# A four-layer hybrid trunk on one core: start order, first weight unit, unit loop, logits order, memory norm and recurrence order changed

## The chip, the cores and the metric

The kernel runs on one core of one Trainium2 chip. The metric is the device time of one execution in microseconds. Inputs and outputs are float32: 256 tokens of width 1024, 256 memory tokens, four layers.

## The reference

Four residual layers; each has a mixer (differential attention, HGRN2 recurrence, chunked SGU, differential attention), a cross-attention into the normed memory and a SwiGLU feed-forward. What the change touches, cut from the reference:

```python
mem_n = rmsnorm(mem, norm_mem)
...
for i in range(DEPTH):
    hn = rmsnorm(x, norm_mix[i])
    mix = (diff_attention, hgrn2, chunked_sgu)[i % 3](hn, ...)
    x = x + mix
    x = x + mem_cross_attention(rmsnorm(x, norm_cross[i]), mem_n, ...)
    x = x + swiglu(rmsnorm(x, norm_ffn[i]), ...)
# diff_attention: 8 heads, two 64-wide q and k per head
lam = exp(sum(lq1 * lk1)) - exp(sum(lq2 * lk2)) + lam_init
p = softmax(logits)                      # logits per head and feature half c
attn = p[:, :, 0] - lam * p[:, :, 1]
# hgrn2: A[t, s] = sum_k q[t] * k[s] * prod of the gates between s and t
```

## The kernel before, in words

**Weights.** All projections stream their weights in units of 1 MB. `load_to` (DMA issue at L116, on the SP queue, which starts transfers in program order) fills a ring of three raw buffers; `split_to` turns a unit into a rounded half `whi` (ScalarE cast, L132) and a remainder `wlo` (VectorE subtract, L133), each in two pieces of 128x1024. One float32 product is three matmuls: high by high, high by low, low by high.

**Two kinds of blocks.** `columns_steps` (L221, L226) takes 256 weight columns per unit and makes transposed results, `join` (L240, L241) copies them out of PSUM. `rows_steps` (L172) takes 256 weight rows per unit and accumulates into four PSUM banks, one for each token tile `t` and column half `n`; in a unit its loops run over `kk`, then `t`, then `n`. Both are generators that yield after each matmul.

**Hand order.** In differential attention and in the recurrence TensorE's order is written by hand: `advance(filler, n)` issues the next n steps of the projections, and between them stand the small pieces, `weigh` (logits at L562, bias and scale L567, softmax L571 to L587), `turn` (transposes of the attention), `near` and `level` of the recurrence. The other engines are ordered by a scheduler, except where `keep_in_program_order` pins an instruction.

**Start.** `run` transposes x in two halves (`norm_half`: sums of squares on ScalarE, L290, and transposes L267 with copies L256, L257) and splits the first unit. The four lambda vectors, each broadcast to 128 partitions, come over ScalarE's queue; two VectorE products use them (L397). `memory` norms mem (sums L290, L417, power on GpSimd L285, scaling L421), transposes it (16 matmuls, L267) and splits it; it is called in layer 0 before the q block.

**Logits.** The two feature halves c sit on partitions 0 to 63 and 64 to 127; for each token tile and head the two halves' matmuls follow each other, into banks `pl0` and `pl1`.

**Recurrence.** `level(lev, hq)` for eight levels and two head quarters (L777 products into `psa`, then L784, L785, L790 scalings and the masked copy L793); `near` prepares the next level's operand `hke` (L750, L752). Single calls of `level` alternate with 9 filler steps.

## Time and profile before

| | |
|---|---|
| median of 3 runs | 1633.71 us (1633.59 to 1634.44) |
| the profiled execution | 1635.31 us, span 1633.6 us |
| matmul records on TensorE | 8221 |
| mean granted TensorE clock | 0.994 |
| HBM traffic | 283 MB, 173 GB/s over the span |

The span is from the first to the last instruction. Slices of the profile's page show TensorE in nine tenths or more of every slice but the first and the last, with the clock at nine tenths or more in every slice but the first; times below are microseconds from the span's start. The clock of a window is in the windows' rows: 1.00 is 2.4 GHz, 0.50 is 1.2 GHz.

### The profile page before, as it was taken

Reading aid. Unit: us, or ns where it says so; the run is one execution under the profiler, and the core shown is the slowest. Engines: PE = TensorE matmul, PEld = TensorE weight load, DVE = VectorE, ACT = ScalarE, POOL = GpSimd, SP = SyncE. Lnnn points to the kernel's source line nnn. Section 1 sums busy time; section 2 is a strip of 40 time slices with the busy share of each in tenths; the row PEclk is TensorE's granted clock in tenths of the full one; section 3 lists DMA queues with packets and bytes.
Section 4 is the critical chain, followed back from the end, with each engine's and each line's share of the span. In section 5 each row is a group of like instructions: output and inputs, shape, how many; then the busy total and the mean of one; then the engine's idle time right before and its main releaser. Section 6 shows DMA issues by size and latency. Waiting matters only on the chain.

```text
span 1633.6 us, 21253 instructions
## 1 busy us (share of the span) xinstructions
PE 1607.5 (98%) x8221; PEld 1359.5 (83%) x8221; DVE 1022.7 (63%) x1482; ACT 880.7 (54%) x1467; POOL 43.5 (3%) x86
## 2 busy tenths in 40 slices
PE   6999999999999999999999999999999999999998
PEld 5788888888888888888888888888888788888886
DVE  5877765554687667555545866555547876665463
ACT  5676554453564656454436655544535765554452
POOL 2000000000000000000000000000000000000000
PEclk8999999999999999999999999999999999999999
DMA  8535445556543454564565554455656455455461
GB/s 290 183 125 192 163 154 181 185 179 203 181 155 104 140 172 154 162 199 155 206 206 170 192 181 155 155 184 165 218 182 205 129 172 186 141 183 183 134 236 68
DMA packets 151253, 282.87 MB, mean 173 GB/s; under 512 B 6390, under 2 KB 79840, under 8 KB 151024
## 3 DMA queue, kind: packets, MB, share of 16 engines
q1 hardware_dynamic: 146368, 275.34, 51.2%
q10 hardware_dynamic: 4320, 4.47, 0.9%
q0 software_dynamic: 464, 1.70, 0.3%
q8 instruction: 64, 1.05, 0.3%
q14 instruction: 37, 0.30, 0.1%
HBM read 280.43 MB, written 2.63 MB: 173 GB/s over the span
## 4 chain that ended last, share of the span: by engine, by line
PE 93%; DVE 1%; ACT 1%; issue 0%; POOL 0%; DVEq 0%; POOLq 0%; ACTq 0%
PE acc L172 67%; PE acc L221 11%; PE acc L226 6%; PE pst L267 3%; PE psa L777 1%; PE pso L980 1%; PE psl L941 1%; PE pl L562 0%; DVE wlo L133 0%; PE pse L964 0%; DVE de L567 0%; DVE dmx L571 0%; PE pso L626 0%; ACT de L577 0%; PE pso L627 0%
## 5 line engine op out<-in xcount | busy, mean ns | idle before, releaser
L133 DVE TENSOR_TENSOR wlo<-wraw,whi 128x1024 fp32r<-128x1024 f32 (+1 forms) x536 | 635.4, 1191 | 439.5 <-ACT whi L132 435.2
L132 ACT CAST whi<-wraw 128x1024 fp32r<-128x1024 f32 (+1 forms) x536 | 547.6, 1026 | 528.4 <-PE acc L172 467.3
L172 PE MATMUL acc<-whi,xs 128*128 128x512 f32 x1728 | 546.2, 393 | 2.2 <-DVE dq L241 2.1
L172 PEld LDWEIGHTS acc<-whi,xs 128*128 128x128 f32 x1728 | 324.4, 188 | 70.4 <-DVE dq L241 3.5
L172 PE MATMUL acc<-wlo,xs 128*128 128x512 f32 x864 | 338.4, 392 | 0.0
L221 PE MATMUL acc<-xs,whi 128*128 128x512 f32 x704 | 251.4, 401 | 7.9 <-ACT whi L132 6.9
L226 PE MATMUL acc<-xs,wlo 128*128 128x256 f32 x704 | 197.7, 284 | 0.0
L172 PEld LDWEIGHTS acc<-wlo,xs 128*128 128x128 f32 x864 | 162.7, 188 | 32.3
L221 PEld LDWEIGHTS acc<-xs,whi 128*128 128x128 f32 x704 | 133.6, 191 | 38.3 <-ACT whi L132 7.1
L172 PE MATMUL acc<-wlo,hh 128*128 128x512 f32 x352 | 137.5, 391 | 0.0
L172 PE MATMUL acc<-whi,hh 128*128 128x512 f32 x352 | 137.4, 392 | 0.0
L226 PEld LDWEIGHTS acc<-xs,wlo 128*128 128x128 f32 x704 | 134.8, 192 | 1.7 <-DVE wlo L133 0.8
L172 PE MATMUL acc<-whi,hl 128*128 128x512 f32 x352 | 112.0, 390 | 0.0
L172 PE MATMUL acc<-wlo,oh 128*128 128x512 f32 x256 | 100.6, 393 | 0.0
L172 PE MATMUL acc<-whi,oh 128*128 128x512 f32 x256 | 100.3, 392 | 0.0
L221 PE MATMUL acc<-m,whi 128*128 128x512 f32 x256 | 89.8, 394 | 0.0
L172 PE MATMUL acc<-whi,ol 128*128 128x512 f32 x256 | 84.8, 392 | 0.0
L172 PE MATMUL acc<-whi,m 128*128 128x512 f32 x256 | 80.7, 392 | 0.0
L172 PEld LDWEIGHTS acc<-whi,hh 128*128 128x128 f32 x352 | 66.1, 188 | 14.4 <-DVE ftmp L1007 1.1
L172 PEld LDWEIGHTS acc<-whi,hl 128*128 128x128 f32 x352 | 66.1, 188 | 13.6
L172 PEld LDWEIGHTS acc<-wlo,hh 128*128 128x128 f32 x352 | 66.1, 188 | 13.4
L226 PE MATMUL acc<-m,wlo 128*128 128x256 f32 x256 | 71.8, 280 | 0.0
(235 smaller groups left out, 1712.7 us busy)
## 6 DMA issues: line engine op xcount, KB each, us to landing
wraw<-in_ffn_w_gu_dram SPq DMA_DIRECT2D x160, 512.0 KB, 4.4
wraw<-in_ffn_w_down_dram SPq DMA_DIRECT2D x44, 1024.0 KB, 4.9
wraw<-in_ca_w_kv_dram SPq DMA_DIRECT2D x32, 1024.0 KB, 5.2
wraw<-in_da_w_in_dram SPq DMA_DIRECT2D x24, 1024.0 KB, 5.2
wraw<-in_ca_w_q_dram SPq DMA_DIRECT2D x16, 1024.0 KB, 5.2
wraw<-in_ca_w_o_dram SPq DMA_DIRECT2D x16, 1024.0 KB, 4.9
wraw<-in_hg_w_in_dram SPq DMA_DIRECT2D x16, 1024.0 KB, 5.5
wraw<-in_da_w_out_dram SPq DMA_DIRECT2D x8, 1024.0 KB, 4.9
```

What stands on the lines that cost most here:

```text
L132: nc.scalar.copy(h, rq)
L133: nc.vector.tensor_tensor(l, rq, h.bitcast(F32), op=ALU.subtract)
L172: nc.tensor.matmul(acc[key], lhsT=x_(k)[:, t * P : (t + 1) * P], rhs=w_[kk][:, 0, c], start=first and j == 0, stop=last and j == 2,)
L221: nc.tensor.matmul(acc[j].rearrange("p (s t) -> p s t", s=2), lhsT=wh[k // 4][:, k % 4, c], rhs=x[:, :, k, :], start=k == 0, stop=False, s ...
L226: nc.tensor.matmul(acc[j][:, 0:256], lhsT=wl[k // 4][:, k % 4, c], rhs=x[:, 0, k, :], start=False, stop=k == 7, skip_group_check=True,)
L267: nc.tensor.transpose(ps[:, i * 256 + t * P : i * 256 + (t + 1) * P], src[:, t, cs * P : (cs + 1) * P], self.ident)
L777: nc.tensor.matmul(ps[:, o : o + 64].rearrange("p (b e) -> p b e", e=half), lhsT=kes[lev % 2][:, h, t * P : (t + 1) * P], rhs=right, start ...
L941: nc.tensor.matmul(ps[:, t * 256 : (t + 1) * 256], lhsT=q_[:, 2 * h + d, t * P : (t + 1) * P], rhs=k_[:, 2 * h + d, :], start=n == 0, stop ...
L980: nc.tensor.matmul(pso[:, d * 256 : (d + 1) * 256], lhsT=v_[:, m, c], rhs=e_[:, h, m, :], start=n == 0, stop=n == 5)
```

## The change

Seven edits. (1) The four lambda transfers go from ScalarE's queue to SP's, behind mem, and the two products are pinned in program order. (2) The first weight unit is loaded by two transfers of 512 KB; the loop's variable `n` is also `load_to`'s argument, so a call stops earlier than asked. (3) `run` transposes both halves of x before any sum of squares. (4) In a unit of `rows_steps` the token tile is the outer loop. (5) The logits' matmuls run by feature half, then token tile. (6) `memory` is called inside the q block of layer 0, after 32 of its steps, with its sums pinned. (7) In the recurrence both head quarters of a level follow each other, then 24 filler steps. What is cut from the diff only moves sums of squares into functions of their own.

```diff
--- before.py
+++ after.py
@@ -113,7 +113,10 @@
             r = self.pw.tile([P, nk, width], F32, tag="raw", bufs=N_RAW, name="wraw")
             o = 0
             for src, cw in parts:
-                nc.sync.dma_start(out=r[:, :, o : o + cw], in_=src.rearrange("(k p) n -> p k n", p=P))
+                n = 2 if self.n_load == 0 else 1
+                for q in range(n):
+                    ks = slice(q * nk // n, (q + 1) * nk // n)
+                    nc.sync.dma_start(out=r[:, ks, o : o + cw], in_=src.rearrange("(k p) n -> p k n", p=P)[:, ks, :])
                 o += cw
             self.raw[self.n_load] = r
             self.n_load += 1
@@ -178,9 +181,9 @@
             if mid is not None and u == at:
                 mid()
             wh, wl = self.next_unit()
-            for kk in range(2):
-                k = 2 * u + kk
-                for t in range(2):
+            for t in range(2):
+                for kk in range(2):
+                    k = 2 * u + kk
                     for n in range(nn):
                         for j in range(2):
                             mm((t, n), k, kk, wh, wl, (j,))
@@ -316,17 +319,17 @@
         self.load_to(N_RAW)
         self.mem = self.slab(3, [P, 2, D], name="mem")
         nc.sync.dma_start(out=self.mem, in_=a["mem"][0].rearrange("(t p) d -> p t d", p=P))
-
         self.st = self.slab(8, [P, 1152], name="start")
+        lq = self.st[:, 0:512].rearrange("p (a l d) -> p a l d", a=4, l=2)
+        for i, n in enumerate(("da_lq1", "da_lk1", "da_lq2", "da_lk2")):
+            nc.sync.dma_start(out=lq[:, i], in_=a[n].partition_broadcast(P))
+
         rel = self.small([8, BUCKETS], "rel", bufs=1)
         nc.gpsimd.dma_start(out=rel, in_=a["rel_bias"])
         tb = self.st[:8, 768:1152]
         nc.gpsimd.memset(tb[:, 256:384], NEG)
         g1 = self.slab(10, [P, P], name="g1")
         nc.scalar.dma_start(out=g1[0:32, :], in_=a["norm_mix"].rearrange("l (c p) -> (l c) p", p=P))
-        lq = self.st[:, 0:512].rearrange("p (a l d) -> p a l d", a=4, l=2)
-        for i, n in enumerate(("da_lq1", "da_lk1", "da_lq2", "da_lk2")):
-            nc.scalar.dma_start(out=lq[:, i], in_=a[n].partition_broadcast(P))
         self.g1b = self.slab(13, [P, P], name="g1b")
         for i, g in enumerate((a["norm_cross"], a["norm_ffn"], a["hg_lower_bounds"])):
             nc.gpsimd.dma_start(out=self.g1b[i * 32 : (i + 1) * 32, :], in_=g.rearrange("l (c p) -> (l c) p", p=P))
@@ -394,7 +397,7 @@
         lq = st[:, 0:512].rearrange("p (a l d) -> p a l d", a=4, l=2)
         pr = st[:, 512:768].rearrange("p (a l d) -> p a l d", a=2, l=2)
         for i in range(2):
-            nc.vector.tensor_tensor(pr[:, i], lq[:, 2 * i], lq[:, 2 * i + 1], op=ALU.mult)
+            self.tc.keep_in_program_order(nc.vector.tensor_tensor(pr[:, i], lq[:, 2 * i], lq[:, 2 * i + 1], op=ALU.mult))
         ls = self.small([P, 4], "lqs", bufs=1)
         nc.vector.tensor_reduce(ls, pr.rearrange("p a l d -> p (a l) d"), axis=AX.X, op=ALU.add)
         nc.scalar.activation(ls, ls, AF.Exp)
@@ -412,7 +415,8 @@
         ss = self.small([P, 2, 2], "ss", bufs=2)
         for t in range(2):
             for n in range(2):
-                self.sumsq(ss[:, t, n : n + 1], self.mem[:, t, n * 512 : (n + 1) * 512])
+                ins = self.sumsq(ss[:, t, n : n + 1], self.mem[:, t, n * 512 : (n + 1) * 512])
+                self.tc.keep_in_program_order(ins)
         st = self.small([P, 2], "sst", bufs=2)
         nc.vector.tensor_reduce(st, ss, axis=AX.X, op=ALU.add)
         r = self.small([P, 2], "rstd", bufs=2)
@@ -531,7 +541,6 @@
         nc.vector.tensor_scalar_mul(sc, rstd, 0.125)
         if l == 0:
             self.more_consts()
-            self.memory()
         aT1 = self.slab(13, [P, 8, 256], name="daT1")
         aT0 = self.slab(14, [P, 8, P], name="daT0")
         s0 = self.small([P, 4, 2, 2], "ds0", bufs=1)
@@ -554,15 +563,16 @@
             mx = self.small([P, 2, 4], "dmx", bufs=3)
             sm = self.small([P, 2, 2, 2], "dsm", bufs=3)
             hs = slice(2 * hp, 2 * hp + 2)
-            for t, w in tiles:
-                lg = [self.ps("pl0"), self.ps("pl1")]
-                for i in range(2):
-                    for c in range(2):
-                        r = slice(c * 64, (c + 1) * 64)
+            lgs = [[self.ps("pl0"), self.ps("pl1")] for _ in tiles]
+            for c in range(2):
+                r = slice(c * 64, (c + 1) * 64)
+                for (t, w), lg in zip(tiles, lgs):
+                    for i in range(2):
                         nc.tensor.matmul(
                             lg[c][:, i * w : (i + 1) * w], lhsT=qt[r, 2 * hp + i, t * P : (t + 1) * P],
                             rhs=kt[r, 2 * hp + i, 0:w], start=True, stop=True,
                         )
+            for (t, w), lg in zip(tiles, lgs):
                 for c in range(2):
                     nc.vector.scalar_tensor_tensor(
                         e[t][:, c], lg[c][:, : 2 * w].rearrange("p (h m) -> p h m", h=2), sc[:, t : t + 1],
@@ -603,8 +613,11 @@
         es = {}
         advance(filler, 16)
         self.load_bias(bias)
+        advance(filler, 16)
+        if l == 0:
+            self.memory()
         for n, act, hp in (
-            (44, weigh, 0), (48, weigh, 1), (8, turn, 0), (32, weigh, 2),
+            (28, weigh, 0), (48, weigh, 1), (8, turn, 0), (32, weigh, 2),
             (8, turn, 1), (28, weigh, 3), (8, turn, 2), (26, turn, 3),
         ):
             advance(filler, n)
@@ -803,20 +816,14 @@
 
         filler = both()
         with self.in_order():
-            advance(filler, 96)
-            near(0, 0)
-            advance(filler, 16)
-            level(0, 0)
-            advance(filler, 24)
-            level(1, 0)
-            advance(filler, 16)
-            near(0, 1)
-            advance(filler, 12)
-            for i in range(14):
-                level(*((i // 2, 1) if i % 2 == 0 else (2 + i // 2, 0)) if i < 12 else (i - 6, 1))
-                if i == 1:
-                    corner()
-                advance(filler, 9 if i < 11 else 16)
+            advance(filler, 128)
+            for hq in range(2):
+                near(0, hq)
+            for lev in range(8):
+                advance(filler, 24 if lev else 18)
+                for hq in range(2):
+                    level(lev, hq)
+            corner()
             advance(filler, 320)
         o = self.slab(9, [P, 2, D], name="ho")
         psos, later = [], []
@@ -1061,9 +1068,13 @@
         self.make_plan()
         self.consts()
         self.begin_norm(5, self.g_mix(0))
-        self.norm_half(0)
-        self.split_to(1)
-        self.norm_half(1)
+        for n in range(2):
+            self.transpose_split(self.x, self.xh, self.xl, [(c, c) for c in range(4 * n, 4 * n + 4)], self.xgain)
+            if n == 0:
+                self.split_to(1)
+        for n in range(2):
+            self.norm_sums(n)
+            self.norm_power(n)
         for l in range(DEPTH):
             mixer = (self.diff_attention, self.hgrn2, self.sgu)[l % 3]
             mixer(l, lambda mid: self.mem_k(l, mid))
```

Line numbers in the pieces of order below are those of each kernel's own file: what is L116, L132, L133, L240, L241 before is L119, L135, L136, L243, L244 now, and L172, L221, L226 are L175, L224, L229.

**VectorE at the start**, before: `start` is the tile with the lambda vectors, `xs` the transposed x, `wraw`, `whi`, `wlo` the weight unit and its parts.

```order
L356 COPY G<-psg 128x32
L397 TENSOR_TENSOR start<-start 128x128 x2
L399 TENSOR_REDUCE lqs<-start 128x4
L257 SCALAR_TENSOR_TENSOR xs<-pst,G,xs 128x256 x3
L133 TENSOR_TENSOR wlo<-wraw,whi 128x1024
L257 SCALAR_TENSOR_TENSOR xs<-pst,G,xs 128x256
L133 TENSOR_TENSOR wlo<-wraw,whi 128x1024
```

The same place now:

```order
L359 COPY G<-psg 128x32
L260 SCALAR_TENSOR_TENSOR xs<-pst,G,xs 128x256
L136 TENSOR_TENSOR wlo<-wraw,whi 128x1024
L260 SCALAR_TENSOR_TENSOR xs<-pst,G,xs 128x256 x2
L136 TENSOR_TENSOR wlo<-wraw,whi 128x1024
L260 SCALAR_TENSOR_TENSOR xs<-pst,G,xs 128x256 x3
L136 TENSOR_TENSOR wlo<-wraw,whi 128x1024
L260 SCALAR_TENSOR_TENSOR xs<-pst,G,xs 128x256 x2
```

The lambda products and their sum stood second; they are gone from here to the end of the key block. **SP at the start**, before:

```order
L309 DMA ident<-in_c_ident_dram 128x128
L313 DMA x<-in_x_dram 128x512 x2
L116 DMA wraw<-in_da_w_in_dram 128x8x256 x3
L318 DMA mem<-in_mem_dram 128x2x1024
L116 DMA wraw<-in_da_w_in_dram 128x8x256 x5
L116 DMA wraw<-in_da_w_in_dram 128x2x1024 x4
```

and now:

```order
L312 DMA ident<-in_c_ident_dram 128x128
L316 DMA x<-in_x_dram 128x512 x2
L119 DMA wraw<-in_da_w_in_dram 128x4x256 x2
L119 DMA wraw<-in_da_w_in_dram 128x8x256
L321 DMA mem<-in_mem_dram 128x2x1024
L325 DMA start<-in_da_lq_dram 128x128
L325 DMA start<-in_da_lk_dram 128x128
L325 DMA start<-in_da_lq_dram 128x128
L325 DMA start<-in_da_lk_dram 128x128
L119 DMA wraw<-in_da_w_in_dram 128x8x256 x6
```

The first unit is two transfers, the third unit stands behind mem and the lambda vectors.

**TensorE and ScalarE in the q block of layer 0**, TensorE before (`g1b` and `g` are gains, `acc` the projections' banks):

```order
L221 MATMUL acc<-xs,whi 128x512
L226 MATMUL acc<-xs,wlo 128x256
L365 MATMUL psg<-ident,g1b 128x96
L369 MATMUL psg<-ident,g_104 128x19
L267 MATMUL pst<-ident,mem 128x128 x16
L221 MATMUL acc<-xs,whi 128x512
L226 MATMUL acc<-xs,wlo 128x256
```

TensorE now:

```order
L224 MATMUL acc<-xs,whi 128x512
L229 MATMUL acc<-xs,wlo 128x256
L224 MATMUL acc<-xs,whi 128x512
L229 MATMUL acc<-xs,wlo 128x256
L270 MATMUL pst<-ident,mem 128x128 x16
L224 MATMUL acc<-xs,whi 128x512
L229 MATMUL acc<-xs,wlo 128x256
```

ScalarE now, around the sums over mem (`dq` is the q block's result, `lbe` and `lqs` belong to bounds and lambda):

```order
L385 ACTIVATE lbe<-lbe 128x32
L135 CAST whi<-wraw 128x1024
L243 COPY dq<-acc 128x256 x2
L293 ACTIVATE junk,ss<-mem 128x512
L135 CAST whi<-wraw 128x1024
L403 ACTIVATE lqs<-lqs 128x4
L293 ACTIVATE junk,ss<-mem 128x512 x3
L259 ACTIVATE m<-pst,G_437 128x256 x8
```

The 16 transposes of mem move from the start of the q block to the end of its first unit; ScalarE's four sums over mem stand behind the copies of that same unit's result.

**VectorE before the first two levels of the recurrence**, before (`hks`, `hk`, `hq`, `hf` are shifted key, key, query, gate; `psa` a level's products):

```order
L724 TENSOR_TENSOR hks<-hk,hf 128x2x255
L241 TENSOR_TENSOR hf<-acc,hf 128x256
L767 TENSOR_TENSOR hb<-hf 128x4x127
L716 TENSOR_TENSOR hf<-hf,rb 128x512
L785 TENSOR_TENSOR hks<-hks,hf 128x4x127
L133 TENSOR_TENSOR wlo<-wraw,whi 128x1024
L719 TENSOR_SCALAR hf<-hf,lb 128x256 x2
L784 TENSOR_TENSOR hq<-hq,hf 128x512
L723 TENSOR_SCALAR hk<-hf 128x512
L793 COPY_PREDICATED hA<-masks,psa 128x256
L724 TENSOR_TENSOR hks<-hk,hf 128x2x255
```

and now:

```order
L737 TENSOR_TENSOR hks<-hk,hf 128x2x255
L729 TENSOR_TENSOR hf<-hf,rb 128x512
L136 TENSOR_TENSOR wlo<-wraw,whi 128x1024
L732 TENSOR_SCALAR hf<-hf,lb 128x256 x2
L798 TENSOR_TENSOR hks<-hks,hf 128x4x127
L736 TENSOR_SCALAR hk<-hf 128x512
L797 TENSOR_TENSOR hq<-hq,hf 128x512
L737 TENSOR_TENSOR hks<-hk,hf 128x2x255
L806 COPY_PREDICATED hA<-masks,psa 128x256 x2
L780 TENSOR_TENSOR hb<-hf 128x4x127
L798 TENSOR_TENSOR hks<-hks,hf 128x4x127
```

The scaling of the first quarter's query (now L797), which rewrites what the first level's matmuls read, stands ahead of the last quarter of shifted keys (now L737).

## Rows read from the trace of the kernel before

**Rows 1.** The page, busy time of TensorE: us (share of the span) x instructions.

```profile
PE 1607.5 (98%) x8221; PEld 1359.5 (83%) x8221; DVE 1022.7 (63%) x1482; ACT 880.7 (54%) x1467; POOL 43.5 (3%) x86
```

**Rows 2.** TensorE's waits, by line and releaser: us in total, times, longest us.

```profile
PE acc L221 <- ACT whi L132: 6.9, 1, 6.9
...
PE acc L172 <- DVE dq L241: 2.1, 2, 1.8
```

**Rows 3.** Timeline of VectorE at the start: start, us, instruction, [idle before <-releaser].

```profile
11.66 0.29 DVE L397 TENSOR_TENSOR start<-start 128x128 f32<-128x128 f32 x1 [4.90 <-DMA start<-in_da_lk_dram]
...
14.21 0.29 DVE L397 TENSOR_TENSOR start<-start 128x128 f32<-128x128 f32 x1 [2.26 <-DMA start<-in_da_lk_dram]
```

**Rows 4.** Timeline of TensorE at the start.

```profile
6.46 3.48 PE L267 MATMUL pst<-ident,x 128*128 128x128 f32 x16
...
16.84 1.22 PE L221 MATMUL acc<-xs,whi 128*128 128x512 f32 x2 [6.90 <-ACT whi L132]
```

**Rows 5.** Windows: busy (x) of PE PEld DVE ACT POOL, clock, DMA, GB/s.

```profile
16.84:23.20 6.36, 6.32 (x19) 4.93 (x20) 5.92 (x11) 6.36 (x13) 1.27 (x2) 0.50 1.08 408
...
23.20:44.00 20.80, 20.80 (x123) 18.11 (x123) 17.84 (x30) 14.03 (x26) 0.70 (x1) 1.00 0.92 296
...
77.90:81.30 3.40, 3.40 (x13) 2.37 (x13) 2.06 (x2) 0.81 (x1) 0.00 (x0) 0.50 0.35 86
...
470.40:473.80 3.40, 3.40 (x12) 2.93 (x12) 3.17 (x7) 0.45 (x1) 0.00 (x0) 0.50 0.07 28
...
1269.00:1271.00 2.00, 1.22 (x7) 0.68 (x5) 2.00 (x7) 2.00 (x6) 0.00 (x0) 1.00 0.00 0
```

**Rows 6.** DMA issues at 2 and 7 us: count, KB, us to landing.

```profile
wraw<-in_da_w_in_dram SPq DMA_DIRECT2D x1, 1024.0 KB, 9.9
...
wraw<-in_da_w_in_dram SPq DMA_DIRECT2D x1, 1024.0 KB, 13.8
...
mem<-in_mem_dram SPq DMA_DIRECT2D x1, 1024.0 KB, 17.7
```

**Rows 7.** Timeline of ScalarE, GpSimd and VectorE, 26 to 33 us (mem's norm).

```profile
26.73 0.63 ACT L290 ACTIVATE junk<-mem 128x512 bf16<-128x512 f32 x1
...
29.66 0.19 ACT L290 ACTIVATION_READ_ACCUMULATOR junk<-mem 128x1 f32 x1
...
30.32 0.70 POOL L285 TENSOR_TENSOR rstd<-rstd,mhalf 128x2 f32<-128x2 f32 x1 [8.85 <-DVE rstd L284]
...
31.05 0.75 DVE L421 TENSOR_SCALAR mem<-mem,rstd 128x1024 f32<-128x1024 f32 x1 [0.47 <-POOL rstd L285]
```

**Rows 8.** Timeline of TensorE around the first logits.

```profile
56.13 0.38 PE L562 MATMUL pl<-dk,dq 64*128 64x128 f32 x2
...
56.13 1.58 PE L562 MATMUL pl<-dk,dq 64*128 64x128 f32 x16
...
57.64 0.50 PE L221 MATMUL acc<-xs,whi 128*128 128x512 f32 x1
```

**Rows 9.** The chain of waits: start us, us, what.

```profile
125.68 1.75 PE pst L267 x16
...
208.54 5.75 PE pso L980 x48
...
266.11 21.80 PE acc L172 x96
...
368.29 52.19 PE acc L172 x230
```

**Rows 10.** Timeline of TensorE, value block of layer 0.

```profile
76.38 0.50 PE L172 MATMUL acc<-whi,xs 128*128 128x512 f32 x1 [1.85 <-DVE dq L241]
```

**Rows 11.** Timeline of the recurrence of layer 1.

```profile
467.69 0.66 ACT L750 COPY hke<-hks 128x512 f32<-128x512 f32 x1
...
468.49 1.97 PE L777 MATMUL psa<-hq,hke 128*128 128x64 f32 x16 [1.71 <-ACT hke L750]
...
470.77 0.68 DVE L784 TENSOR_TENSOR hq<-hq,hf 128x512 f32<-128x512 f32 x1
```

More of the change, by code (lines that the diff above doesn't have):

```diff
@@ L289, in sumsq @@
         junk = self.small([P, 512], "junk", dt=BF16, bufs=1)
-        self.nc.scalar.activation(junk[:, : src.shape[1]], src, AF.Square, accum_out=acc)
+        return self.nc.scalar.activation(junk[:, : src.shape[1]], src, AF.Square, accum_out=acc)
     def set_rows(self):
@@ L432, in norm_half, with norm_sums, norm_power @@
     def norm_half(self, n):
+        self.norm_sums(n)
+        self.transpose_split(self.x, self.xh, self.xl, [(c, c) for c in range(4 * n, 4 * n + 4)], self.xgain)
+        self.norm_power(n)
+    def norm_sums(self, n):
         for t in range(2):
             self.sumsq(self.xss[:, t, n : n + 1], self.x[:, t, n * 512 : (n + 1) * 512])
-        self.transpose_split(self.x, self.xh, self.xl, [(c, c) for c in range(4 * n, 4 * n + 4)], self.xgain)
+    def norm_power(self, n):
         if n == 1:
@@ L1063, in run @@
         self.begin_norm(5, self.g_mix(0))
-        self.norm_half(0)
-        self.split_to(1)
-        self.norm_half(1)
+        for n in range(2):
+            self.transpose_split(self.x, self.xh, self.xl, [(c, c) for c in range(4 * n, 4 * n + 4)], self.xgain)
+            if n == 0:
+                self.split_to(1)
+        for n in range(2):
+            self.norm_sums(n)
+            self.norm_power(n)
         for l in range(DEPTH):
```

## The prediction

> **What bounds the kernel now.** The page's first section comes first: TensorE is busy for 1607.5 of 1633.6 us [rows 1]. So only three things move the time: TensorE's few waits, the stretches at half clock, and the number of TensorE slots. The waits' view shows that the largest wait, 6.9 us, comes once, for the first weight cast [rows 2]; the next are 2.1 us for a copy out of PSUM. The timelines and windows then give each place its price. VectorE stands 4.90 and 2.26 us in front of the lambda products [rows 3], and all that it does for TensorE is behind them; TensorE ends its transposes of x at 9.9 and starts on weights at 16.84 [rows 4]. Half clock shows in windows after such idles: 0.50 from 16.84 to 23.20, for 3.4 us from 77.90 and for 3.4 us from 470.40 [rows 5]. A window in which TensorE was idle for 0.78 of 2 us kept 1.00 [rows 5]. So an idle of about 1 us costs itself, one of 1.7 us or more another 1.7 us (3.4 us at half speed).
>
> The sums are made against the profiled execution, 1635.3 us; the median of the runs is 1.6 lower. A change within 0.2%, 3.3 us, can't be told from none.
>
> **Start (lambda, halves, transposes first): -5.0.** Without the lambda products VectorE makes its part of xs as transposes end. The whole first unit landed at 2.2 + 9.9 = 12.1 [rows 6]; its first half should be there by 9 to 10. TensorE starts at about 10 instead of 16.84, but the 6.8 us aren't all kept, since the third unit now stands behind mem and the lambda vectors. It landed at 6.6 + 13.8 = 20.4; mem, which had its place in the queue, at 7.1 + 17.7 = 24.9 [rows 6]. I take 24.9 for the third unit, the row of the same place; the ends are 22 (the lambda packets, which may have slowed the first units, now come later) and 27 (they are added ahead of it). Two units are 64 matmuls and 10.8 us at full clock (32 in 5.4 us by the second window [rows 5]), 3.2 more for the half clock at the start, so that TensorE is through with them at about 25, when the third has only landed; its cast and subtraction hold it to about 26 to 27, an idle of 1 to 2 us. Two more units of 5.4 us and half a fall of the clock end the key block at 38 to 39.5 instead of 43.7, where the mem transposes began. Gain 5.0, bounds 2 and 7.5.
>
> **Memory in the q block: +9.2.** Before, the norm of mem ran beside the key block: four sums at 0.77 from 26.73 to 29.85, GpSimd 0.70, scalings of 0.75 from 31.05 [rows 7], the transposes far behind. Now TensorE's order has the transposes directly behind q's first unit, the sums are pinned behind the copies of that unit's result, and nothing else stands on TensorE between. From the unit's last matmul: copies 0.7, the first sum, a cast of 1.0 that lies between, three more sums (3.1 for all four), then 2.0 from the last sum's end to the second of two scalings, by [rows 7] 1.2 to the first scaling and 0.75 each: 0.7 + 1.0 + 3.1 + 1.2 + 1.5 is 7.5, less the little that runs side by side: 7.2 idle. Behind so long an idle comes half clock, 3.4 us at half speed and some already in the transposes, which are at 0.109 each when warm (16 in 1.75 [rows 9]): I take 2.4. The old placement had 0.4 of small waits there. Sum 9.2; the ends are 5 (no cast between, full clock) and 12 (casts of other units come between, two falls).
>
> **Logits by feature half: +1.1 for each of eight, +8.8.** The first two records, one of each half, start together in one entry of 0.38 us [rows 8]: the two feature halves run at the same time. The 16 records of one `weigh`, eight with 128 columns and eight with 256, take 57.64 - 56.13 = 1.51 us [rows 8], that is eight pairs. In the new order four records, in two tiles, of the same half follow each other before any of the other half, so only the switch in the middle can overlap. A 128-column transpose has a slot of 1.75/16 = 0.109 [rows 9]; four pairs at that and four at twice that are 1.31, the other 0.2 is entry and exit. If a lone record keeps a pair's slot, the 1.31 become 2.62, less 0.2 at the switch: +1.1. If a lone one were faster, like the 256-column matmuls at 5.75/48 = 0.12 [rows 9], it would be +0.5 each, +4.3 in all. Above, without overlap at the switch, +10.4. I take 8.8, since nothing in the rows shows a lone record with fewer slots. The Trainium skill (TensorE: Matmul & The Clock Gate, "Why this matters for your kernels") says that matmuls with few rows run concurrently only in distinct row groups and that a single one takes as long as one with all rows; by it the sum is the upper value, +8.8 to +10.4, and no run here shows a lone one.
>
> **Token tile outside: value block of layer 0, -2.5; elsewhere 0.** The second pair of accumulators is needed after 12 instead of 6 matmuls, 1.4 us later at 52.19/230 = 0.227 each [rows 9]. The wait of 1.85 at 76.38 for a PSUM copy [rows 10] shrinks to about 0.5, too little for the fall of the clock that followed (1.7 [rows 5]); some 0.8 may come back in the next unit. Bounds -4 and +1.5. Elsewhere no accumulator is waited for. Stretches of whole blocks and of unit bodies alone have the same spacing, 21.80/96 = 0.227 and 0.227 [rows 9], so the order of the loops shows no price. The layer-3 twin of the wait stands before a columns block, which is not reordered: 0.
>
> **Recurrence: +1.8.** Now TensorE waits 1.71 us before the first level [rows 11], then runs at half clock [rows 5]: 3.0 in all with what the clock costs beyond cover. In the new order the first level of the first quarter is followed at once by that of the second. For this VectorE must first rescale the first quarter's query, 0.68 [rows 11], which waits for the first quarter's matmuls; behind it comes the last quarter of shifted keys, about the same, and then ScalarE copies it, 0.66 [rows 11], behind two shorter copies. 0.68 + 0.7 + 0.66 + 0.6 and the hand-overs between are 3.2 idle, and the clock falls: 4.9 against 3.0. Between later levels stand 24 filler matmuls, 5.4 us, enough for the two rescalings and copies if the casts give way; the bounds, 0 and +4, hold a small wait there.
>
> **Sum.** -5.0 + 9.2 + 8.8 - 2.5 + 1.8 = +12.3: 1647.6 profiled, 1646 as the median. With the terms' bounds drawn half way, 1640 to 1652.
>
> **Rivals.** *Token order quickens the whole stream* (faster). 3768 of 4800 row-block matmuls stand in unit bodies. If writing one token tile's banks for longer spared 4.3 ns of the 227, it would give 16 us back, enough to pass 1630.4; at 3.3 ns it cancels the rest. Against it: a stretch with bodies alone (368.29) and stretches with tails, which already keep one bank, are equal to 0.3 ns [rows 9]. At 5 ns: 1646 - 19 = 1627. Chance 0.10. *Logits cost little*: a lone record takes half a pair's slot, and the term is 0 to +4: 1637 to 1641. For it, a 256-column matmul at 0.12; against it, that one is of another type with all rows. 0.12. *The memory chain is short or covered*: the scheduler's casts give way and the clock stays, or the mem sums run earlier: 9.2 becomes 0 to 3, 1637 to 1640. For it, mem lands long before; against it, the order on ScalarE. 0.08. *The third unit lands late*, at 27 or after, the fourth with it, and the clock falls once more; with a second fall around the memory: +6, 1652 to 1658. 0.10. *The change doesn't do what it says*: were the first half unit no earlier than 12.1, the start would gain 2 instead of 5, and the time be 1649; this lies in the forecast's range.
>
> **The numbers.** The forecast with its range has 0.60. The range 1635 to 1654 adds the cheap logits and most of the short chain and of the late third unit; outside stay the quick stream and the end of the late one. Faster: 0.10, the quick stream alone. Same (1630.4 to 1637.0): 0.10, half of the cheap logits and half of the short chain, where the start or the value block at its better bound takes 2 or so more. Slower: 0.80.
>
> **What would show it.** The first weight matmul at about 10; a wait of some 7 us for VectorE's scaling of mem in front of the 16 transposes at about 44, with half clock behind it; 16 logit records in 2.6 us instead of 1.51; no fall of the clock near 77; a wait of about 3 us inside the first level at about 470; 0.227 in long stretches. A wait before the mem transposes under 3 us, logits under 2 us, or a spacing below 0.224 would make the prediction wrong.

## The result, and the profile after

The changed kernel takes 1642.99 us (median of 6 runs, 1642.0 to 1643.84) against 1633.89 of the kernel before on the same chip: a ratio of 1.0053, 95% interval 1.0042 to 1.0063, 9.1 us slower. The forecast was 1646 with a range of 1635 to 1654, slower. The profiled execution took 1643.25 us with a span of 1641.5, 7.9 above the span before.

TensorE's waits in the changed kernel (us in total, times, longest), to be held against [rows 2]:

```profile
PE pst L270 <- DVE mem L425: 8.3, 2, 8.1
PE psg L358 <- DMA g<-in_norm_mix_dram: 6.6, 1, 6.6
PE psa L790 <- ACT hke L763: 2.8, 1, 2.8
PE acc L229 <- DVE wlo L136: 1.3, 2, 0.8
PE acc L175 <- DVE dq L244: 1.1, 1, 1.1
PE acc L224 <- ACT whi L135: 0.8, 1, 0.8
PE acc L224 <- DVE dq L244: 0.8, 1, 0.8
```

The 6.9 us before the first weight matmul are gone; 8.1 us before the transposes of mem are new, the recurrence's wait grew from 1.7 to 2.8, and the wait for the PSUM copy in the value block shrank from 1.85 [rows 10] to 1.1. The second line, 6.6 us for the norm gain ahead of the first transposes, stood in the waits' view of before too, with 6.2; the change leaves it as it is.

The mem chain in the timelines of ScalarE, GpSimd, VectorE and TensorE, changed kernel (start us, us, instruction, [idle before <- releaser]):

```profile
45.16 0.64 ACT L243 COPY dq<-acc 128x256 f32<-128x256 f32 x2
45.68 0.64 ACT L293 ACTIVATE junk<-mem 128x512 bf16<-128x512 f32 x1
...
46.31 1.04 ACT L135 CAST whi<-wraw 128x1024 fp32r<-128x1024 f32 x1
...
47.68 0.61 ACT L293 ACTIVATE junk<-mem 128x512 bf16<-128x512 f32 x1
...
49.70 0.19 ACT L293 ACTIVATION_READ_ACCUMULATOR junk<-mem 128x1 f32 x1
...
50.67 0.70 POOL L288 TENSOR_TENSOR rstd<-rstd,mhalf 128x2 f32<-128x2 f32 x1 [29.46 <-DVE rstd L287]
...
51.41 1.42 DVE L425 TENSOR_SCALAR mem<-mem,rstd 128x1024 f32<-128x1024 f32 x2 [0.81 <-POOL rstd L288]
...
43.82 0.28 PE L229 MATMUL acc<-xs,wlo 128*128 128x256 f32 x1
52.22 0.48 PE L270 MATMUL pst<-ident,mem 128*128 128x128 f32 x1 [8.12 <-DVE mem L425]
```

Each step of the forecast's chain is there: the copies of q's first unit, a sum, a cast between, three sums, the power, the scaling. One cast more, at 44.22, stands ahead of the copies and adds 1.0; on the other side TensorE starts behind the first of the two scalings. So the wait is 8.1 and not 7.2.

The chain inside the first level of the recurrence, in the timelines of VectorE, ScalarE and TensorE:

```profile
479.71 0.69 DVE L797 TENSOR_TENSOR hq<-hq,hf 128x512 f32<-128x512 f32 x1 [0.23 <-PE psa L790]
480.32 0.68 DVE L737 TENSOR_TENSOR hks<-hk,hf 128x510 f32<-128x510 f32 x1
...
480.66 1.20 ACT L765 COPY hke<-hk 128x512 f32<-128x512 f32 x2
481.75 0.66 ACT L763 COPY hke<-hks 128x512 f32<-128x512 f32 x1
...
482.47 2.95 PE L790 MATMUL psa<-hq,hke 128*128 128x64 f32 x16 [2.79 <-ACT hke L763]
```

The first quarter's query is scaled, then the last quarter of shifted keys is made, then ScalarE copies it behind two shorter copies, and TensorE waits for that copy, as forecast. The windows at the first weights and at both waits show the clock (the column behind the busy times):

```profile
10.10:12.20 2.10, 2.10 (x8) 1.64 (x8) 2.03 (x4) 1.80 (x4) 1.80 (x7) 1.00 1.10 342
...
44.10:52.20 8.10, 0.00 (x0) 0.00 (x0) 7.08 (x23) 5.51 (x14) 0.70 (x1) 0.64 0.86 308
52.20:56.00 3.80, 3.60 (x17) 3.31 (x17) 1.93 (x4) 1.79 (x5) 0.00 (x0) 0.50 0.59 238
...
483.30:490.10 6.80, 6.80 (x23) 5.74 (x23) 3.89 (x6) 2.05 (x3) 0.00 (x0) 0.50 0.01 2
```

The 16 transposes of mem ran at half clock, 3.8 us from 52.22 to 56.0 against 1.75 [rows 9] at full clock. Behind the recurrence's wait TensorE ran at half clock for 6.8 us. Start and logits in TensorE's timeline:

```profile
10.17 1.20 PE L224 MATMUL acc<-xs,whi 128*128 128x512 f32 x2
...
31.50 0.49 PE L224 MATMUL acc<-xs,whi 128*128 128x512 f32 x1 [0.81 <-ACT whi L135]
32.76 0.39 PE L229 MATMUL acc<-xs,wlo 128*128 128x256 f32 x1 [0.76 <-DVE wlo L136]
...
38.28 0.40 PE L224 MATMUL acc<-xs,whi 128*128 128x512 f32 x1
...
61.40 2.13 PE L571 MATMUL pl<-dk,dq 64*128 64x128 f32 x16
63.46 0.50 PE L224 MATMUL acc<-xs,whi 128*128 128x512 f32 x1
```

Weights start at 10.17 instead of 16.84 [rows 4], and q's first unit, the next after the key block, starts at 38.28. The 16 logit records take 63.46 - 61.40 = 2.06 us where they took 1.51 [rows 8].

Where the time went, from the starts of the same TensorE instruction in both timelines:

| TensorE reaches | before | after | difference |
|---|---|---|---|
| first weight matmul | 16.84 | 10.17 | -6.67 |
| first logits, layer 0 | 56.13 | 61.40 | +5.27 |
| first attention times values, layer 0 | 103.52 | 108.07 | +4.55 |
| first transposes, layer 1 | 420.31 | 424.62 | +4.31 |
| first recurrence products times values | 544.03 | 550.73 | +6.70 |
| first logits, layer 3 | 1261.72 | 1267.87 | +6.15 |
| first attention times values, layer 3 | 1306.65 | 1314.47 | +7.82 |
| last matmul's end | 1625.90 | 1633.44 | +7.54 |

The first +5.27 splits in two. The key block is over at 38.28, where q's first unit starts; before, it was over at 43.38, where the transposes of mem start in TensorE's timeline:

```profile
43.38 1.09 PE L267 MATMUL pst<-ident,mem 128*128 128x128 f32 x8
```

That is a gain of 5.1. The rest, 10.4, is mem.

### The profile page after: what moved, and what is told of

Same layout as the page of the kernel before. It is cut to its first block, busy times and chain, and to the rows that moved or that the text cites. A ratio compares the mean times of both kernels' runs of the same rounds, so it can differ in the third digit from the quotient of the medians.

```text
span 1641.5 us, 21259 instructions
## 1 busy us (share of the span) xinstructions
PE 1611.5 (98%) x8221; PEld 1363.5 (83%) x8221; DVE 1022.1 (62%) x1482; ACT 881.6 (54%) x1467; POOL 43.8 (3%) x86
## 4 chain that ended last, share of the span: by engine, by line
PE 93%; ACT 1%; DVE 0%; issue 0%; POOL 0%; DVEq 0%; POOLq 0%; ACTq 0%
PE acc L175 66%; PE acc L224 11%; PE acc L229 6%; PE pst L270 3%; PE psa L790 2%; PE pso L987 1%; PE psl L948 1%; PE pl L571 1%; PE pse L971 0%; ACT de L587 0%; PE pso L639 0%; PE pso L640 0%; PE pso L638 0%; PE pat L609 0%; PE psm L903 0%
## 5 line engine op out<-in xcount | busy, mean ns | idle before, releaser
L136 DVE TENSOR_TENSOR wlo<-wraw,whi 128x1024 fp32r<-128x1024 f32 (+1 forms) x536 | 634.6, 1191 | 439.8 <-ACT whi L135 422.5
L135 ACT CAST whi<-wraw 128x1024 fp32r<-128x1024 f32 (+1 forms) x536 | 547.0, 1027 | 545.5 <-PE acc L175 475.3
L175 PE MATMUL acc<-whi,xs 128*128 128x512 f32 x1728 | 545.8, 393 | 1.1 <-DVE dq L244 1.1
L175 PEld LDWEIGHTS acc<-whi,xs 128*128 128x128 f32 x1728 | 325.0, 188 | 69.3 <-DVE dq L244 1.5
L175 PE MATMUL acc<-wlo,xs 128*128 128x512 f32 x864 | 337.9, 391 | 0.0
L224 PE MATMUL acc<-xs,whi 128*128 128x512 f32 x704 | 248.6, 398 | 1.7 <-ACT whi L135 0.8
L229 PE MATMUL acc<-xs,wlo 128*128 128x256 f32 x704 | 196.1, 282 | 1.3 <-DVE wlo L136 1.3
L175 PEld LDWEIGHTS acc<-wlo,xs 128*128 128x128 f32 x864 | 162.9, 189 | 32.6
L224 PEld LDWEIGHTS acc<-xs,whi 128*128 128x128 f32 x704 | 131.9, 189 | 32.2 <-ACT whi L135 1.5
L175 PE MATMUL acc<-whi,hh 128*128 128x512 f32 x352 | 137.4, 390 | 0.0
L175 PE MATMUL acc<-wlo,hh 128*128 128x512 f32 x352 | 137.3, 390 | 0.0
L229 PEld LDWEIGHTS acc<-xs,wlo 128*128 128x128 f32 x704 | 133.0, 189 | 3.4 <-DVE wlo L136 2.4
L175 PE MATMUL acc<-whi,hl 128*128 128x512 f32 x352 | 111.3, 390 | 0.0
L175 PE MATMUL acc<-wlo,oh 128*128 128x512 f32 x256 | 100.5, 393 | 0.0
L175 PE MATMUL acc<-whi,oh 128*128 128x512 f32 x256 | 100.1, 391 | 0.0
L224 PE MATMUL acc<-m,whi 128*128 128x512 f32 x256 | 89.6, 394 | 0.0
L175 PE MATMUL acc<-whi,ol 128*128 128x512 f32 x256 | 84.8, 392 | 0.0
L175 PE MATMUL acc<-whi,m 128*128 128x512 f32 x256 | 80.7, 391 | 0.0
L175 PEld LDWEIGHTS acc<-whi,hl 128*128 128x128 f32 x352 | 66.1, 188 | 13.6
L175 PEld LDWEIGHTS acc<-wlo,hh 128*128 128x128 f32 x352 | 66.1, 188 | 13.5
L175 PEld LDWEIGHTS acc<-whi,hh 128*128 128x128 f32 x352 | 66.1, 188 | 13.5
L229 PE MATMUL acc<-m,wlo 128*128 128x256 f32 x256 | 71.3, 278 | 0.0
```

Source lines behind the costliest of these rows:

```text
L135: nc.scalar.copy(h, rq)
L136: nc.vector.tensor_tensor(l, rq, h.bitcast(F32), op=ALU.subtract)
L175: nc.tensor.matmul(acc[key], lhsT=x_(k)[:, t * P : (t + 1) * P], rhs=w_[kk][:, 0, c], start=first and j == 0, stop=last and j == 2,)
L224: nc.tensor.matmul(acc[j].rearrange("p (s t) -> p s t", s=2), lhsT=wh[k // 4][:, k % 4, c], rhs=x[:, :, k, :], start=k == 0, stop=False, s ...
L229: nc.tensor.matmul(acc[j][:, 0:256], lhsT=wl[k // 4][:, k % 4, c], rhs=x[:, 0, k, :], start=False, stop=k == 7, skip_group_check=True,)
```

## The experiments

All are changes to the changed kernel unless said otherwise. Ratios are to the kernel before on the same chip, to be held against 1.0053; spans are of one profiled execution each, to be held against 1641.5. Three things blur the spans. The kernel before took 1633.9 us beside the changed kernel and 1635.2 to 1635.8 beside the variants, so that a difference of spans is 1.3 to 1.9 off where the ratio is not. The start varies: with everything ahead of it unchanged, q's first unit ended at 44.1 in the changed kernel's profile and at 42.3 to 43.4 in those of six variants; the fourth unit landed 17.3 us after its issue in the first and 12.3 in two of the others. And the half clock behind the recurrence's wait varies: with the same order and the same wait of 2.79 it lasted 6.8 us in the changed kernel and 3.4 with alternating logits,

```profile
481.25:484.65 3.40, 3.40 (x12) 2.92 (x12) 2.25 (x4) 1.02 (x2) 0.00 (x0) 0.50 0.00 0
```

so that the stretch from layer 1's first transposes to its first products times values took 126.1 and 124.7 us. Spans are therefore read to about 2 us, and marks inside the kernel are used below.

**Memory before the q block.**

```diff
-                ins = self.sumsq(ss[:, t, n : n + 1], self.mem[:, t, n * 512 : (n + 1) * 512])
-                self.tc.keep_in_program_order(ins)
+                self.sumsq(ss[:, t, n : n + 1], self.mem[:, t, n * 512 : (n + 1) * 512])
...
             self.more_consts()
+            self.memory()
...
-        advance(filler, 16)
-        if l == 0:
-            self.memory()
...
-            (28, weigh, 0), (48, weigh, 1), (8, turn, 0), (32, weigh, 2),
+            (44, weigh, 0), (48, weigh, 1), (8, turn, 0), (32, weigh, 2),
```

> The changed kernel with the memory norm, sums unpinned, called before the q block again (first logits after 44 steps). Theory: the wait of 8.12 us in front of the mem transposes and the half clock behind it, 10.0 us together, belong to the call's place alone; span 1641.5 - 10 = 1631.5, median near 1633. Rival: the wait only takes the place of another (weights of the q block come late, or ScalarE's other rows wait in its stead); then at most half comes back, span 1636 or more, with a new wait of 3 us or more between 38 and 60 us.

Span 1631.7, ratio 0.9985 (0.9975 to 0.9995). The first logits come at 51.35 instead of 61.40, 10.0 us sooner; the spans give 9.8 and the ratios 11. So the memory part costs what the changed kernel's trace shows. One wait of 1.85 us is left before the transposes, since VectorE has the scalings late.

**Only the norm of mem early.** Sums, power and scaling become a function of their own, `memory_norm`, which is called before the q block without the pin on the sums; transposes and split stay inside the block.

```diff
-                self.tc.keep_in_program_order(ins)
...
             self.more_consts()
+            self.memory_norm()
```

> The changed kernel with mem's sums, power and scaling issued before the q block, and only its transposes and their split after 32 steps. Theory: the 8 us wait is the chain of sums behind the copies of q's first unit, and the place of the transposes costs nothing: a wait under 0.5 us in front of them, full clock behind, span 10 us shorter than the changed kernel's, 1630.5 to 1632. With the call before the q block 1.85 us of wait were left, since VectorE scaled mem late; a unit further on that should be covered. Rival: the wait goes with the place (something else that TensorE needs at this point is late): 2 us or more remain.

Span 1630.0, ratio 0.9983 (0.9973 to 0.9993). TensorE's timeline has no gap ahead of the transposes:

```profile
42.42 0.28 PE L229 MATMUL acc<-xs,wlo 128*128 128x256 f32 x1
42.54 2.24 PE L270 MATMUL pst<-ident,mem 128*128 128x128 f32 x16
44.54 0.47 PE L224 MATMUL acc<-xs,whi 128*128 128x512 f32 x1
```

So TensorE doesn't wait at the transposes in their new place; only ahead of the first logits is there 0.5 us that wasn't there before:

```profile
PE pl L574 <- DVE m L260: 0.5, 1, 0.5
```

What cost 10 us was the norm issued, and pinned, behind q's first unit. Which of the two, the place of the call or the pin, holds the sums back is not separated: both runs take away both.

**Logits alternating again.**

```diff
-            for c in range(2):
-                for (t, w), lg in zip(tiles, lgs):
-                    for i in range(2):
+            for (t, w), lg in zip(tiles, lgs):
+                for i in range(2):
+                    for c in range(2):
```

> The changed kernel with the logits' matmuls alternating between the feature halves again. The 16 records of one call take 2.06 us in the changed kernel's trace against 1.51 before. Theory: 8 x 0.55 = 4.4 us come back, span 1637.1. The prediction's own size would be 8.8, span 1632.7. Rival: VectorE, which needs both halves, hides part of it, so that under 2 us come back, span over 1639.5.

Span 1636.1, ratio 1.0024 (1.0014 to 1.0033). From first logits to first attention product the layers take 45.22 and 44.59 us, against 46.67 and 46.60: 1.45 and 2.0 back, 3.5 together. Of the rest of the 5.4 between the spans, 1.5 is the start and 1.4 the recurrence with its shorter half clock; 1.0 goes the other way in the stretches without logits. The 16 records take 1.51 us in each of the eight calls and 2.06 in the changed kernel, 4.4 in all. 0.9 of it doesn't reach the marks: 0.36 stands in a new wait ahead of a transpose of the attention in layer 0, 0.2 in a longer one for a PSUM copy in layer 3, and the rest isn't accounted for. So the term is neither the prediction's 8.8 nor the rival's 2. The ratios give 4.7, with about 2 either way.

**Two more orders, to see how the halves overlap.** First runs of four (token tile, then half), then runs of eight with the wide tile first.

```diff
-            for c in range(2):
-                for (t, w), lg in zip(tiles, lgs):
+            for (t, w), lg in zip(tiles, lgs):
+                for c in range(2):
```

> The changed kernel with the logits by token tile, then feature half: four records of one half, then four of the other. In the changed kernel's trace the second half's first record started when the fifth of the eight of the first half did, with three of them still to come. Theory (the array takes up a record of the other half while at most three of this half wait): the second half starts one slot after the first, 16 records take 1.5 to 1.75 us. Rival (records start strictly in order): 4 x 0.109 alone, then overlap only at each switch, 2.3 to 2.6 us.

```diff
-                for (t, w), lg in zip(tiles, lgs):
+                for (t, w), lg in reversed(list(zip(tiles, lgs))):
```

> The changed kernel with the wide token tile first: eight records of one half (four of 256 columns, four of 128), then eight of the other. Theory (look-ahead counted in records): the second half starts when the fifth record of the first half does, now after 4 x 0.217 = 0.87 us instead of 0.55; 16 records take 2.06 + 0.32 = 2.35 to 2.45 us. Rival (look-ahead in time, or overlap by what the banks allow): as long as in the changed kernel, 2.06.

TensorE's timeline with runs of four:

```profile
60.94 1.68 PE L571 MATMUL pl<-dk,dq 64*128 64x128 f32 x16
62.55 0.50 PE L224 MATMUL acc<-xs,whi 128*128 128x512 f32 x1
```

and with the wide tile first:

```profile
61.60 2.55 PE L571 MATMUL pl<-dk,dq 64*128 64x256 f32 x16
64.07 0.50 PE L224 MATMUL acc<-xs,whi 128*128 128x512 f32 x1
```

They take 62.55 - 60.94 = 1.61 and 64.07 - 61.60 = 2.47 us (spans 1638.8 and 1645.2, one execution each). Both fit a look-ahead counted in records, the second 0.02 above its range; the strict order and the look-ahead in time are out. In the trace with the wide tile first, the other half's first record started 0.974 us behind the first of all, with the fifth of this half's (0.968).

**The recurrence's order of before.**

```diff
-            advance(filler, 128)
...
-                advance(filler, 24 if lev else 18)
-                for hq in range(2):
-                    level(lev, hq)
-            corner()
+            advance(filler, 96)
+            near(0, 0)
...
+            for i in range(14):
+                level(*((i // 2, 1) if i % 2 == 0 else (2 + i // 2, 0)) if i < 12 else (i - 6, 1))
+                if i == 1:
+                    corner()
+                advance(filler, 9 if i < 11 else 16)
```

> The changed kernel with the recurrence's order of before (single levels between 9 filler steps). Theory: the difference of the two traces between the start of the layer-1 block and the end of its products, 2.4 us, comes back: span 1639.1, a wait near 1.7 us in front of the first level. Rival: the wait in the grouped order comes from the units' loop order or the late start and not from the grouping: span 1641 or more.

Span 1639.8, ratio 1.0035 (1.002 to 1.005). A miss: from layer 1's first transposes to its first products times values it takes 125.55 us, the changed kernel 126.11, the kernel before 123.72. The 0.6 that came back of the 2.4 is less than the same stretch varies by its half clock. The waits show why no more did:

```profile
PE psa L790 <- ACT hke L763: 1.7, 1, 1.7
PE psd L755 <- DVE qk L753: 1.5, 1, 1.5
```

The wait of before is there, and a second one for the corner's small product, which VectorE makes behind a scaling and a masked copy here. This run can't price the grouping.

**Grouped, but the first level apart.**

```diff
                 for hq in range(2):
                     level(lev, hq)
+                    if lev == 0 and hq == 0:
+                        advance(filler, 24)
```

> The changed kernel with the recurrence still grouped, but 24 filler steps between the two quarters of the first level. Theory: the wait of 2.79 us in front of the second quarter goes, and with it the half clock behind (about 1.9 us lost): span 4 to 5 us shorter, 1636.5 to 1637.5, or 1 less where the start is quicker. Rival: VectorE's work for a level is the limit, and the next level waits in its stead: 1639.5 or more, with a wait over 1 us between 480 and 550.

Span 1635.5, ratio 1.0012 (1.0003 to 1.0021). The same stretch takes 121.19 us, 4.9 less than the changed kernel and 2.5 less than the kernel before; no wait for `hke` is left, and the clock stays full:

```profile
476.00:490.00 14.00, 14.00 (x80) 12.12 (x79) 12.75 (x20) 8.46 (x12) 0.00 (x0) 1.00 0.45 151
```

The grouping costs nothing at seven levels; its whole price is two adjacent quarters at the first. Against the 124.7 of the trace in which the half clock lasted 3.4 us the gain is 3.5.

**kk outside in the units.**

```diff
-            for t in range(2):
-                for kk in range(2):
+            for kk in range(2):
+                for t in range(2):
```

> The changed kernel with kk outside and the token tile inside in a unit, as before. Theory: the wait for the PSUM copy in the value block of layer 0 grows from 1.06 to 1.9 us or more and the clock falls again: span 2.5 to 3.5 us longer, 1644.0 to 1645.0; spacing in long stretches stays 0.227. Rival (the token order quickens the stream): 0.5 us or less in layer 0, and the rest spread over all row blocks, spacing above 0.228, 1644 or more as well, but with no wait at 80 us. Third: no difference, 1641.5, the wait having gone for other reasons.

Span 1645.1, ratio 1.0069 (1.0053 to 1.0085). Its value-block wait and the clock behind:

```profile
PE acc L175 <- DVE dq L244: 2.2, 1, 2.2
```

```profile
83.00:90.00 7.00, 7.00 (x31) 5.16 (x30) 3.82 (x7) 1.04 (x1) 0.00 (x0) 0.76 0.33 114
```

From first logits to first attention product it takes 49.60 us against 46.67: the token order is worth 2.9 there. Behind this stretch the kernel is 1.2 longer in all, in pieces of 0.1 to 0.5 from mark to mark, which is no more than these stretches differ between kernels with one loop order. In a window of 100 us inside one feed-forward (300 to 400) TensorE started 456 matmuls in this order and 457 in the other, so the stream as such is no faster.

**The start: lambda, and the halves.** The first try put the lambda transfers back on ScalarE's queue where they are issued in the changed kernel, ahead of the norm gain.

```diff
-            nc.sync.dma_start(out=lq[:, i], ...)
+            nc.scalar.dma_start(out=lq[:, i], ...)
-            self.tc.keep_in_program_order(nc.vector.tensor_tensor(pr[:, i], ...))
+            nc.vector.tensor_tensor(pr[:, i], ...)
```

> The changed kernel with the lambda transfers on ScalarE's queue and the products not pinned; VectorE then has them at its head again. Theory: VectorE waits for them until about 14, the first weight matmul comes back to 16 to 17 (10.2 in the changed kernel), half clock for 6 us behind it, and the start's whole gain is lost: span 4.5 to 6 us longer than the changed kernel's, 1646 to 1647.5. Rival: the halves carry the gain; the first weight matmul stays under 13 and the span under 1643.5.

Span 1647.7, ratio 1.0082 (1.0067 to 1.0097), but not for the reason given. TensorE's largest wait:

```profile
PE psg L358 <- DMA g<-in_norm_mix_dram: 14.8, 1, 14.8
```

The gain landed behind the lambda vectors and held the first transposes. A second try issues them behind the gain, as the kernel before does:

```diff
         nc.scalar.dma_start(out=g1[0:32, :], ...)
+        for i, n in enumerate(("da_lq1", ...)):
+            nc.scalar.dma_start(out=lq[:, i], ...)
```

> The changed kernel with the lambda transfers on ScalarE's queue behind the norm gain, as before the change, and the products not pinned. (With them ahead of the gain, TensorE's first matmul waited for the gain until 14.8.) Theory: the products hold VectorE until 12 to 14, the first weight matmul comes at 14 to 17 with half clock behind, and the key block ends 4 to 6 us later: span 1644.5 to 1647. Rival: the halves carry the gain, first weight matmul under 12 and span under 1643.5.

Span 1643.5, ratio 1.0068 (1.005 to 1.0087). The first weight matmul comes at 14.02, half clock follows (0.50 from 14.00 to 20.00), and q's first unit ends at 48.73, 4.6 later than in the changed kernel's profile and 5 to 6 later than in the six variants. The lambda products held the start: TensorE waits for VectorE's part of xs, and VectorE for the lambda vectors. TensorE's wait, then VectorE's timeline:

```profile
PE acc L224 <- DVE xs L260: 3.9, 1, 3.9
...
10.39 0.29 DVE L400 TENSOR_TENSOR start<-start 128x128 f32<-128x128 f32 x1 [3.46 <-DMA start<-in_da_lk_dram]
12.73 0.29 DVE L400 TENSOR_TENSOR start<-start 128x128 f32<-128x128 f32 x1 [2.04 <-DMA start<-in_da_lk_dram]
```

The second half of the first unit landed at 14.2 instead of 10.7 too, with the lambda packets on their way at the same time; how much of the 4.6 that makes is not separated. The span rose by 2.0 only, less than the theory gave, since the wait for mem shrank from 8.1 to 6.5 and the recurrence's stretch, with the shorter half clock, from 126.1 to 124.5. The last run of this part loads the first unit whole:

```diff
-                n = 2 if self.n_load == 0 else 1
-                for q in range(n):
+                for q in range(1):        # one transfer; load_to goes as far as asked
```

> The changed kernel with the first weight unit in one transfer, and the load calls as far ahead as asked (third unit ahead of mem). Theory: the first cast waits for the whole unit until about 11 to 12, the first weight matmul comes at 12 to 13.5 and the idle ahead of it brings half clock for a few us; the key block ends 1 to 3 us later, since later units wait for less: span 1642 to 1644.5. Rival: the later units' landing sets the end of the key block alone; the late start is absorbed, span 1640.3 to 1641.5.

Span 1641.7, ratio 1.0049 (1.0033 to 1.0065), between the two answers. Weights start at 11.76, 1.6 later; q's first unit ends at 44.67, 0.6 later than in the changed kernel, in both with a late fourth unit (landed 16.4 us after its issue here; TensorE waits 0.57 us for it at 31.62). Against the 42.96 of a trace in which that unit landed early, the halves, together with the load calls that stop earlier, are worth at most about 1.7 us; which of the two answers holds stays open.

**Three parts mended.** Early norm, alternating logits, split first level together.

> The changed kernel with three parts mended: mem's norm before the q block and only its transposes inside it, alternating logits, 24 filler steps inside the first recurrence level. Theory (the prices add, each from its own place): from the 1630.0 us span of the kernel with the early norm, 3.5 less for the logits and 4.9 less for the recurrence, span 1621.6, median near 1623.5, 0.7% below the kernel before. Rival: the prices overlap (a wait covered by one cost shows once the cost is gone, as in the value block of layer 0): span 1624.5 or more, with a new wait of 1 us or more in layer 0 or 3.

Median 1625.74, ratio 0.9942 (0.9929 to 0.9955): 9.4 us faster than the kernel before and, by the ratios, some 18 faster than the changed one. Its span of 1624.5 is 2.9 above the sum, right at the rival's edge: the prices don't quite add. TensorE's waits there:

```profile
PE psg L358 <- DMA g<-in_norm_mix_dram: 6.7, 1, 6.7
PE acc L229 <- DVE wlo L136: 1.3, 2, 0.8
PE acc L224 <- DVE dq L244: 1.0, 1, 1.0
PE pl L574 <- DVE m L260: 0.9, 1, 0.9
```

Recurrence (121.12) and layer 3 (44.57) gave what they should. Layer 0 did not: from first logits to first attention product 46.39, against 46.60 with the early norm alone, so 0.2 of 1.45; the wait for mem's split at the first logits grew from 0.5 to 0.9. The start took 1.0 more (first logits at 50.55 against 49.57), with weights that landed late again (a wait of 0.75 at 32.22) and 0.4 of wait ahead of the transposes of mem. The rest is spread over the stretches between.

## Why the prediction was right, point by point

- **Start, -5.0: measured -5.1.** The first cause is right: without the lambda products at VectorE's head weights start at 10.17, with them at 14.02. The size is right in part by luck, as two of its pieces missed and offset each other. The half rate of the first units, priced at 3.2 us, lasted only to about 12.2 and cost about 0.7: the first eight matmuls take 2.1 us where four pairs at 0.35 take 1.4. (The granted clock reads 1.00 from 10.10 to 12.20 already, though these matmuls are still spaced as at half clock.) The third unit landed at 22.7, not 24.9, and TensorE didn't wait for it; it was the fourth unit's landing at 30.4 that made TensorE wait, 0.81 and 0.76 us at 31.50 and 32.76. A unit took 5.7 us, not 5.4, and the old end of the key block that the gain is counted from is 43.38, not 43.7. What the third edit, both transposes of x ahead of the sums, adds by itself is not shown.
- **Memory, +9.2: measured +10.4.** Shown by both memory runs. The chain was laid out rightly; one cast more stood ahead of it.
- **Logits, +8.8: measured +4.4 in slots, 3.5 net.** This is the term that was mis-sized. The step that failed: "only the switch in the middle can overlap", taken as 0.2 us. (It is eight records of one half that follow each other, four matmuls of two records each, not four.) The other half's records started when five of the eight of this half had started, and then both ran side by side to the end of the first. The lower bound, +4.3, was the one to take, though for another reason: a lone record did keep a pair's slot, 0.11 us with 128 columns and 0.216 with 256, and all the gain is overlap. A 128-column transpose with all 128 rows has a slot of 0.109 [rows 9]. The Trainium skill's rule (TensorE: Matmul & The Clock Gate, "Why this matters for your kernels") that a single matmul with few rows takes as long as one with all rows agrees with this trace. The Trainium skill (TensorE: Matmul & The Clock Gate, Part 3, "What overlaps and what doesn't") also has matmuls start strictly in program order, and there the trace doesn't agree: a record of the second half started at 61.957, the sixth of the first half only at 62.170.
- **Token tile outside, -2.5 in layer 0: measured -2.9.** The reversed order brings wait and clock fall back. The wait shrank to 1.06, not to 0.5, and the 0.8 that was to come back in the next unit didn't. Elsewhere 0 was forecast; 1.1 us less was measured, in three stretches (0.25, 0.55 and 0.29). That this is the loop's is not shown: such stretches differ by 0.8 to 1.5 between kernels with the same loops.
- **Recurrence, +1.8: measured +2.4.** The chain is the forecast one, its wait 2.79 of the forecast 3.2. Shown by the split first level, not by the old order. The size hangs on the clock: with the half clock of 6.8 us it is +2.4, with that of 3.4 in the run with alternating logits +0.9.
- **Sum, +12.3: measured +7.9 in the span, +9.1 in the medians.** The 4.4 between forecast and span are as much as the logits' 4.4; the smaller pieces (-1.1), the value block (-0.4) and layer 3's slightly shorter wait (-0.2) stand against the larger terms of memory (+1.2) and recurrence (+0.6), and that they cancel is luck.

Of the signs that the prediction named, all came but one: 16 logit records took 2.06 us, not 2.6, just above the 2 that it would have counted against itself. One reading of its first paragraph is wrong without touching the sum: the second largest wait of before is the 6.2 us for the norm gain, not 2.1.

The rivals: the quick stream was out (456 and 457 matmuls in 100 us). The third unit was not late; the fourth was, in some executions, at about 1 us. The cheap logits came out in size, +3.5 to +4.4 for 0 to +4, but not for their reason, since a lone record keeps its slot. The short memory chain was out, with 8.1 us of wait, and the first half unit did land early, at 8.6 us.

## What to carry to other kernels

A small computation off the path must be issued so that it ends before the bound engine reaches its user; issued and pinned behind a unit of that engine's own work it cost its whole chain (10 us here), while the user's place cost 0.5 at most. Matmuls on disjoint rows should alternate, or stand in runs of at most four records: runs of eight made 2.06 to 2.47 us of 1.51. Two pieces of a dependent chain that share a scaling engine want filler between them where their operands are late; here that was one level of eight.

## What the hardware showed that was not expected

TensorE doesn't hold to program order across row halves. The 16 records took 1.51 us in runs of two (the alternating order, two records for each matmul), 1.61 in runs of four, 2.06 in runs of eight, and 2.47 with the wide tile first; in these traces the other half's first record started as soon as no more than three records of this half were still to start. The two halves can be told apart in the trace where one is at its 256-column records and the other still at 128.

The clock did not fall after every idle of this length, nor for as long each time. After 1.85 us in the value block of before [rows 10] it was 0.50 for 3.4 us [rows 5]; after 1.85 us ahead of the mem transposes, in the kernel with memory before the q block, and after 1.71 us in the recurrence, in the kernel with the old order there, the next 7 us show

```profile
43.00:50.00 7.00, 7.00 (x47) 6.22 (x46) 7.00 (x20) 5.79 (x12) 0.00 (x0) 1.00 0.98 349
...
471.40:478.40 7.00, 7.00 (x46) 6.32 (x46) 6.24 (x12) 3.34 (x6) 0.00 (x0) 1.00 0.30 118
```

In the kernel before, the same 1.71 us at the same place were followed by 0.50 for 3.4 us [rows 5]; behind 2.79 us it was 3.4 or 6.8 us. So the prediction's price of 1.7 us for an idle of 1.7 or more is one value of several, 0, 1.7 and 3.4, and not a rule.
